# Seven block products for eight in half of a decoder layer's input projection

## The chip, the cores and the metric

The kernel runs on one core of a Trainium2 chip. The metric is the device time of one execution in microseconds (us): before the change the median of three runs is 1809.89 us (1809.57 to 1810.76). The engines are named as the profile names them: PE is TensorE (matmul), PEld its weight loads, DVE is VectorE, ACT is ScalarE, POOL is GpSimd, SP is SyncE, which here only issues DMAs.

## The reference

One layer of a hybrid decoder over 1024 tokens of 2048 channels, in float32. What bears on the change is the first matmul:

```python
def hybrid_layer(x, pre_w, post_w, w_in, ...):
    h = rms_norm(x, pre_w)          # 1024 x 2048
    proj = h @ w_in                 # 2048 x 6016: 47 columns of 128
    za, zb, zc, zd, gate = jnp.split(proj, SPLITS, axis=-1)
    ya = rwkv7_mixer(token_shift(za, mu), ...)   # columns 0 to 12, a scan over the tokens
    yb = swa_sink_attention(zb, sinks)           # 13 to 18
    yc = pool_mixer(zc, pool_w, pool_scale)      # 19 to 22
    yd = spatial_gating(zd, ...)                 # 23 to 30
    y = jnp.concatenate([ya, yb, yc, yd], axis=-1) * jax.nn.silu(gate)   # gate: 31 to 46
    return x + rms_norm(y @ w_out, post_w)
```

RMSNorm divides a token's channels by their root mean square, so its factor (`rstd`) is one number per token, and needs all of the token's channels.

## The kernel before

**Tiling.** The tokens are worked in two halves of 512. The projection makes, for one half, one "column" at a time: 128 output channels x 512 tokens in one PSUM bank, summed over 16 blocks of 128 input channels (`proj`, line 260). Float32 accuracy comes from splitting each operand into a rounded part `hi` and the rest `lo` (`split`, line 161: ScalarE rounds into `wh`, VectorE subtracts into `wl`), and from three matmuls per block (lines 273 to 275: hi x hi, hi x lo, lo x hi), each 128x128 against 128x512. A column so takes 48 matmuls, here called products, and 4 weight splits of 128x512. The split tiles have 3 buffers each, raw weights 3 buffers of 512 KB, and the column's PSUM pool `ps_pj` 2 banks.

**Stages.** `first_half` (line 198) loads and splits the first half of x, and makes columns 12, 0, 4 and 8 at once, while the squares of x are summed for `rstd` (lines 171 to 196). `mixers(0)` (line 876) runs the four mixers of the first half; each mixer is a generator that asks for a column and is stepped once for every column made (the RWKV heads twice). In the first half `rstd` is multiplied in when a column is taken from PSUM (line 889). `out_proj(0)` (line 794) multiplies by `w_out`: 4 x 4 x 16 x 3 = 768 products without other TensorE work, while `second_half` (line 237) scales and splits the second half of x. Then come `mixers(1)` and `out_proj(1)`, and a tail of the last residual rows.

**What sets the order.** A list scheduler places the instructions of each engine when the kernel is built: it takes them as they become ready, by their place in the program, with weight loads and splits ahead (`high_priority`). Each engine then runs its own list strictly in that order. So the RWKV head's work on VectorE (lines 337 to 406, a DMA round trip, the small triangular solve of lines 417 to 421, the chain over 8 chunks of 64 tokens in lines 518 to 545) stands in one list with the weight splits that TensorE's next products wait for.

## Time and profile before

| | us |
|---|---|
| median of 3 runs | 1809.89 |
| the profiled execution's own time | 1808.09 |
| its span, first to last instruction | 1806.3 |
| until the first product | 11.5 |
| from there until the fifth column starts | 52.7 |
| the rest of the first half's projection and mixers | 666.1 |
| output projection, first half | 178.5 |
| projection and mixers, second half | 703.9 |
| output projection, second half | 182.8 |
| tail | 10.8 |

The busy time of an engine is the union of its instructions; an operation that waits in an engine's list is not busy. A matmul's own duration (0.39 us) overlaps with the next one's, so the distance from start to start says what a product costs. PEclk is the clock that TensorE was granted: 1.00 is 2.4 GHz, 0.50 is 1.2 GHz.

### The profile page before, as it was taken

How to read it: one execution, taken by the hardware profiler on the slowest of the kernel's cores; microseconds unless marked ns; L12 is line 12 of the kernel's file. 1: busy time of each engine (PE TensorE's matmuls, PEld its weight loads, DVE VectorE, ACT ScalarE, POOL GpSimd, SP SyncE). 2: the span in 40 equal slices, each digit the busy share in tenths (PEclk: the TensorE clock that was granted, in tenths of full speed). 3: DMA queues.
4: the chain of work that ended last, by engine and by line, in shares of the span. 5: the costliest groups of instructions: out<-in, count | busy, mean ns of one | idle time of the engine just before them, and what ended most of it. 6: DMA issues, size and time to landing. Idle time of an engine off the chain costs nothing.

```text
span 1806.3 us, 26854 instructions
## 1 busy us (share of the span) xinstructions
PE 1754.0 (97%) x10352; PEld 1344.7 (74%) x10352; DVE 988.4 (55%) x2186; ACT 614.9 (34%) x1205; POOL 347.8 (19%) x506
## 2 busy tenths in 40 slices
PE   7999999999999999999999999999999999999997
PEld 5787677767767777788887876677677678778875
DVE  6654677576456644753345457754763564463335
ACT  6333333433333322533233243333333323242230
POOL 4111232022034310110002213311220220100002
PEclk9899999999998999999999999999999999999999
DMA  6242123223323312454343533352232132224445
GB/s 207 91 120 78 59 66 86 70 62 101 105 71 107 114 59 71 145 169 123 123 126 101 174 111 94 103 152 70 73 110 71 59 100 74 71 82 128 140 137 201
DMA packets 58144, 190.00 MB, mean 105 GB/s; under 512 B 8400, under 2 KB 8400, under 8 KB 58016
## 3 DMA queue, kind: packets, MB, share of 16 engines
q1 hardware_dynamic: 44672, 147.34, 26.5%
q0 software_dynamic: 13200, 40.91, 8.0%
q8 instruction: 81, 1.33, 0.3%
q14 instruction: 47, 0.39, 0.1%
q10 hardware_dynamic: 144, 0.03, 0.0%
HBM read 168.86 MB, written 18.87 MB: 104 GB/s over the span
## 4 chain that ended last, share of the span: by engine, by line
PE 83%; DVE 9%; issue 3%; DMA 3%; ACT 1%; POOL 1%; DVEq 0%; SPq 0%; POOLq 0%; ACTq 0%
PE ps_pj L273 18%; PE ps_pj L274 17%; PE ps_pj L275 17%; PE ps_pj L779 3%; PE ps_pj L781 3%; PE ps_pj L780 3%; PE ps_pr L780 3%; PE ps_pr L781 3%; PE ps_pr L779 3%; DVE wl L163 1%; PE ps_pr L401 1%; PE ps_pr L444 1%; DVE ftmp L419 1%; PE ps_y L515 1%; PE ps_ot L653 1%
## 5 line engine op out<-in xcount | busy, mean ns | idle before, releaser
L163 DVE TENSOR_TENSOR wl<-wr,wh 128x512 fp32r<-128x512 f32 x488 | 344.2, 706 | 507.2 <-ACT wh L162 490.6
L273 PE MATMUL ps_pj<-g,wh 128*128 128x512 f32 x1472 | 601.5, 409 | 11.7 <-ACT g L212 11.6
L275 PE MATMUL ps_pj<-g,wl 128*128 128x512 f32 x1472 | 593.6, 403 | 5.7 <-DVE wl L163 5.7
L274 PE MATMUL ps_pj<-g,wh 128*128 128x512 f32 x1472 | 594.0, 404 | 0.0
L162 ACT CAST wh<-wr 128x512 fp32r<-128x512 f32 x488 | 301.6, 620 | 849.7 <-PE ps_pj L274 618.9
L273 PEld LDWEIGHTS ps_pj<-g,wh 128*128 128x128 f32 x1472 | 280.9, 191 | 84.1 <-ACT g L212 11.7
L275 PEld LDWEIGHTS ps_pj<-g,wl 128*128 128x128 f32 x1472 | 280.4, 190 | 74.5 <-DVE wl L163 7.4
L274 PEld LDWEIGHTS ps_pj<-g,wh 128*128 128x128 f32 x1472 | 280.7, 191 | 67.4 <-issue 5.3
L526 POOL TENSOR_SCALAR SD<-g,g 64x64 f32<-64x64 f32 x128 | 63.6, 497 | 502.6 <-DVE g L539 347.5
L779 PE MATMUL ps_pj<-wh,g 128*128 128x512 f32 x224 | 88.5, 395 | 0.5 <-DVE g L889 0.3
L780 PE MATMUL ps_pr<-wl,g 128*128 128x512 f32 x224 | 88.4, 395 | 0.0
L781 PE MATMUL ps_pr<-wh,g 128*128 128x512 f32 x224 | 88.3, 394 | 0.0
L780 PE MATMUL ps_pj<-wl,g 128*128 128x512 f32 x224 | 88.3, 394 | 0.0
L781 PE MATMUL ps_pj<-wh,g 128*128 128x512 f32 x224 | 88.3, 395 | 0.0
L779 PE MATMUL ps_pr<-wh,g 128*128 128x512 f32 x224 | 88.2, 394 | 0.0
L821 POOL DMA_DIRECT2D dram_o<-g x24 | 13.0, 541 | 245.8 <-DVE g L791 242.5
L889 DVE TENSOR_TENSOR g<-ps_pj,g 128x512 f32<-128x512 f32 x45 | 30.9, 687 | 45.6 <-PE ps_pj L275 44.9
L419 DVE TENSOR_TENSOR ftmp<-t,LB 64x1 f32<-64x1 f32 (+14 forms) x120 | 46.1, 384 | 16.8 <-DMA LB<-dl 13.6
L539 DVE SCALAR_TENSOR_TENSOR g<-ps_ch,g,SD 64x64 f32<-64x64 f32 x112 | 31.7, 283 | 34.6 <-PE ps_ch L536 29.9
L779 PEld LDWEIGHTS ps_pj<-wh,g 128*128 128x128 f32 x224 | 42.2, 188 | 11.0 <-DVE g L889 0.7
L779 PEld LDWEIGHTS ps_pr<-wh,g 128*128 128x128 f32 x224 | 42.2, 188 | 10.6 <-DVE g L791 0.8
L781 PEld LDWEIGHTS ps_pj<-wh,g 128*128 128x128 f32 x224 | 42.1, 188 | 9.8
(239 smaller groups left out, 2071.9 us busy)
## 6 DMA issues: line engine op xcount, KB each, us to landing
wr<-in_w_in SPq DMA_DIRECT2D x188, 512.0 KB, 3.8
wr<-in_w_out SPq DMA_DIRECT2D x64, 512.0 KB, 3.6
g<-in_xT POOLq DMA_DIRECT2D x32, 256.0 KB, 6.1
g<-in_x POOLq DMA_DIRECT2D x32, 256.0 KB, 4.6
out_y<-g SPq DMA_DIRECT2D x32, 256.0 KB, 4.0
dram_o<-g POOLq DMA_DIRECT2D x24, 256.0 KB, 3.6
g<-dram_o POOLq DMA_DIRECT2D x24, 256.0 KB, 4.0
g<-in_xT SPq DMA_DIRECT2D x16, 256.0 KB, 5.9
```

Source lines behind the costliest of these rows:

```text
L162: self.nc.scalar.copy(out=hi, in_=raw)
L163: self.nc.vector.tensor_tensor(out=lo, in0=raw, in1=hi.bitcast(F32), op=ALU.subtract)
L273: nc.tensor.matmul(p, hi[:, kk], hh, start=k == 0, stop=False)
L274: nc.tensor.matmul(p, hi[:, kk], hl, start=False, stop=False)
L275: nc.tensor.matmul(p, lo[:, kk], hh, start=False, stop=k == KT - 1)
L419: nc.vector.tensor_tensor(out=tmp[:, 0:i, 0:i], in0=T16[:, 0:i, 0:i].rearrange("p j c -> p c j"), in1=LB[:, 0:i, i].unsqueeze(1).to_broadc ...
L526: nc.gpsimd.tensor_scalar(out=SD[H[h]], in0=SV[h][H[h], c], scalar1=E[H[h], c, C:C + 1], scalar2=None, op0=ALU.mult)
L539: nc.vector.scalar_tensor_tensor(out=SV[h][H[h], c + 1], in0=pt[H[h], 2], scalar=E[H[h], c, C:C + 1], in1=SD[H[h]], op0=ALU.mult, op1=ALU.add)
L779: nc.tensor.matmul(p, yh[:, ms], hi, start=k == 0, stop=False)
L780: nc.tensor.matmul(p, yh[:, ms], lo, start=False, stop=False)
L781: nc.tensor.matmul(p, yl[:, ms], hi, start=False, stop=k == KT - 1)
L889: self.nc.vector.tensor_tensor(out=t, in0=p, in1=self.rstd[0], op=ALU.mult)
```

## The change

The input channels are cut in two halves of eight blocks. For channel blocks 8 to 15 the projection stays as it was, column by column and half by half (24 products a column). For blocks 0 to 7 it is done ahead of all mixers and for both token halves at once, in the scheme of Strassen and Winograd: two columns (m1, m2), two channel quarters and two token halves form a 2 x 2 block product, and seven block products of 12 matmuls stand for eight. The weights' sums and differences (`combine`) are made per pair on VectorE, those of x once (`operands`); 23 pairs and one single column (`solo`, four block products) make the 47 columns. Their results wait in DRAM (`part`), and `column` loads one and adds it as it takes the column's other half from PSUM. Since `rstd` of both token halves is needed for this, x of the second half is loaded at the start as well; meanwhile the other channel half of 12 columns of the first token half is made (`AHEAD`) and also stored to DRAM (`rest`).

```diff
+KH = 4
+SK = 2 * KH
+AHEAD = (12, 0, 4, 8, 1, 5, 9, 2, 6, 10, 3, 7)
+SOLO = 12
...
-        self.gp = pool("gen", 78)
-        self.wrp = pool("wraw", 3)
+        self.gp = pool("gen", 66)
+        self.wrp = pool("wraw", 5)
+        self.wsp = pool("wsum", 4)
+        self.evp = pool("evac", 5)
...
+        self.part = [[self.dpc.tile([P, T], F32, name=f"part{m}_{hf}") for hf in range(NHALF)] for m in range(MT)]
+        self.rest = {m: self.dpc.tile([P, T], F32, name=f"rest{m}") for m in AHEAD}
...
-    def first_half(self):
+    def begin(self):
...
+        for k in range(SK, KT):
+            if k in (SK, SK + 4):
+                self.early[AHEAD[(k - SK) // 4]] = self.w_load(AHEAD[(k - SK) // 4], 1)
             with self.tc.high_priority():
+                xb.append(self.x_load(0, k, nc.sync))
...
+        self.xa = [[], []]
+        with self.tc.high_priority():
+            self.xa[0] = [self.x_load(0, k, nc.sync) for k in range(SK)]
         accs = [self.g(), self.g()]
...
         rstd = self.x_rstd(0, accs)
-        for m, pl in ((12, self.ps_pj), (0, self.ps_pj), (4, self.ps_pr), (8, self.ps_pr)):
-            self.ahead[m] = self.proj(m, pl)
+        held = []
+        def evacuate():
+            m, p = held.pop(0)
+            t = self.tile(self.evp, [P, T], "ev")
+            nc.vector.tensor_tensor(out=t, in0=p, in1=self.rstd[0], op=ALU.mult)
+            nc.gpsimd.dma_start(out=self.rest[m], in_=t)
+        for i, m in enumerate(AHEAD):
+            held.append((m, self.proj(m, (self.ps_pj, self.ps_pr)[i // 2 % 2])))
+            if i == 2:
                 for _ in rstd:
                     pass
+                accs = [self.g(), self.g()]
+                xb = []
+                for k in range(KT):
+                    x = self.x_load(1, (k + SK) % KT, nc.sync)
+                    if k >= KT - SK:
+                        self.xa[1].append(x)
+                    self.x_square(k, x, accs)
+            if i >= 2:
+                evacuate()
+            if i == 5:
+                for _ in self.x_rstd(1, accs):
+                    pass
+                self.operands()
+        while held:
+            evacuate()
+
+    def operands(self):
+        nc = self.nc
+        names = ("b11", "b21", "b22", "t1", "t2", "t3", "t4")
+        self.ops = {n: [] for n in names}
+        for kk in range(KH):
+            b11, b21, b12, b22 = (self.xa[hf][kk + KH * i] for hf in range(2) for i in range(2))
+            for hf, (x, y) in enumerate(((b11, b21), (b12, b22))):
+                for t, k in ((x, kk), (y, kk + KH)):
+                    nc.vector.scalar_tensor_tensor(out=t, in0=t, scalar=self.v["pre_norm_w"][:, k:k + 1],
+                                                   in1=self.rstd[hf], op0=ALU.mult, op1=ALU.mult)
+            t1, t2, t4 = self.g(), self.g(), self.g()
+            nc.vector.tensor_tensor(out=t1, in0=b12, in1=b11, op=ALU.subtract)
+            nc.vector.tensor_tensor(out=t2, in0=b22, in1=t1, op=ALU.subtract)
+            t3 = b12
+            nc.gpsimd.tensor_tensor(out=t3, in0=b22, in1=b12, op=ALU.subtract)
+            nc.gpsimd.tensor_tensor(out=t4, in0=b21, in1=t2, op=ALU.subtract)
+            for n, x in zip(names, (b11, b21, b22, t1, t2, t3, t4)):
+                hi, lo = self.g(dt=F32R), self.g(dt=F32R)
+                self.split(x, hi, lo)
+                self.ops[n].append((hi, lo))
+
+    def strassen(self):
+        nc, tt = self.nc, self.nc.vector.tensor_tensor
+        def combine(op, a, b):
+            with self.tc.high_priority():
+                s = self.tile(self.wsp, [P, T], "ws")
+                tt(out=s, in0=a, in1=b, op=op)
+            return s
+        def product(p, w, name, first):
+            with self.tc.high_priority():
+                hi = self.tile(self.whp, [P, KH, P], "wh", F32R)
+                lo = self.tile(self.wlp, [P, KH, P], "wl", F32R)
+                self.split(w, hi.rearrange("p a b -> p (a b)"), lo.rearrange("p a b -> p (a b)"))
+            for kk, (hh, hl) in enumerate(self.ops[name]):
+                last = kk == KH - 1
+                nc.tensor.matmul(p, hi[:, kk], hh, start=first and kk == 0, stop=False, skip_group_check=True)
+                nc.tensor.matmul(p, hi[:, kk], hl, start=False, stop=False, skip_group_check=True)
+                nc.tensor.matmul(p, lo[:, kk], hh, start=False, stop=last, skip_group_check=True)
+        def evac():
+            return self.tile(self.evp, [P, T], "ev")
+        def copy(p):
+            t = evac()
+            nc.scalar.copy(out=t, in_=p)
+            return t
+        def store(m, hf, t):
+            nc.gpsimd.dma_start(out=self.part[m][hf], in_=t)
+        def add(c, p, m, hf):
+            tt(out=c, in0=p, in1=c, op=ALU.add)
+            store(m, hf, c)
+        def pair(m1, m2):
+            r1, r2 = self.w_load(m1, 0), self.w_load(m2, 0)
+            a11, a12, a21, a22 = r1[:, 0], r1[:, 1], r2[:, 0], r2[:, 1]
+            x, y, z = self.ps(self.ps_pj), self.ps(self.ps_pr), self.ps(self.ps_ot)
+            product(x, a11, "b11", True)
+            c1 = copy(x)
+            product(z, a12, "b21", True)
+            add(c1, z, m1, 0)
+            yield
+            s1 = combine(ALU.add, a21, a22)
+            s2 = combine(ALU.subtract, s1, a11)
+            product(x, s2, "t2", False)
+            c2 = copy(x)
+            product(y, s1, "t1", True)
+            s3 = combine(ALU.subtract, a11, a21)
+            product(x, s3, "t3", False)
+            c3 = copy(x)
+            add(c3, y, m2, 1)
+            yield
+            s4 = combine(ALU.subtract, a12, s2)
+            product(y, s4, "b22", False)
+            add(c2, y, m1, 1)
+            product(x, a22, "t4", False)
+            store(m2, 0, copy(x))
+        def solo(m):
+            r = self.w_load(m, 0)
+            x, z = self.ps(self.ps_pj), self.ps(self.ps_ot)
+            product(x, r[:, 0], "b11", True)
+            c1 = copy(x)
+            product(z, r[:, 1], "b21", True)
+            add(c1, z, m, 0)
+            product(x, r[:, 0], "t1", False)
+            product(x, r[:, 1], "b22", False)
+            store(m, 1, copy(x))
+        solo(SOLO)
+        ms = [m for m in range(MT) if m != SOLO]
+        before = None
+        for i in range(0, len(ms), 2):
+            now = pair(ms[i], ms[i + 1])
+            next(now)
+            if before is not None:
+                for _ in before:
+                    pass
+            next(now)
+            before = now
+        for _ in before:
+            pass
...
-    def second_half(self):
+    def half_input(self, hf):
...
-        for k in range(KT + 2):
-            if k < KT:
-                xs.append(self.x_load(1, k))
+        h, xs, n = [], [], KT - SK
+        for i in range(n + 2):
+            if i < n:
+                xs.append(self.x_load(hf, SK + i))
...
     def proj(self, m, pl=None):
...
-        for half in range(2):
-            raw = self.ahead.pop((m, half), None) or self.w_load(m, half)
-            for q in range(2):
...
+        raw = self.early.pop(m, None) or self.w_load(m, 1)
+        for q in range(2):
...
+    def column(self, hf, m):
+        with self.tc.high_priority():
+            part = self.tile(self.evp, [P, T], "ev")
+            self.nc.sync.dma_start(out=part, in_=self.part[m][hf])
+        t = self.g()
+        if hf == 0 and m in self.rest:
+            self.nc.sync.dma_start(out=t, in_=self.rest[m])
+            self.nc.gpsimd.tensor_tensor(out=t, in0=t, in1=part, op=ALU.add)
+        else:
+            self.nc.vector.tensor_tensor(out=t, in0=self.proj(m), in1=part, op=ALU.add)
+        return t
...
             def proj(r):
-                p = self.ahead.pop(r.want, None) or self.proj(r.want)
-                if hf == 0:
-                    t = self.g()
-                    self.nc.vector.tensor_tensor(out=t, in0=p, in1=self.rstd[0], op=ALU.mult)
-                    p = t
-                r.want = r.gen.send(p)
+                r.want = r.gen.send(self.column(hf, r.want))
...
     def run(self):
-        self.first_half()
+        self.begin()
...
-        self.mixers(0, self.x_stats(1), 30)
-        ssq = self.out_proj(0, self.second_half())
+        self.strassen()
+        for _ in self.half_input(0):
+            pass
+        self.mixers(0, iter(()), 30)
+        ssq = self.out_proj(0, self.half_input(1))
         self.mixers(1, self.finish(0, ssq), 4)
         self.out_proj(1)
```

`x_load` loses its rule on queues (x of both halves now goes over SP at the start, over POOL in `half_input`), the 32 loads of x for the second half become 16 at the start and 8 later (8 more for the first half), and in the tail a few tiles move from the pool `gen` to the new pools `evac` and `wsum`.

**Where instructions move.** In the changed program the lines have other numbers: L409 to L411 are the products of `proj`, L302 to L304 those of `product`, L175 is the VectorE half of `split` (L163 before), L200 and L206 are the small matmuls of `x_rstd` (lines 188 and 194 before), L424 is the addition in `column`.

TensorE before, at the end of the fourth column, which was made ahead (`ps_pr_518`), and at the start of the fifth:

```order
L273 MATMUL ps_pr_518<-g_225,wh_571 128x512
L274 MATMUL ps_pr_518<-g_226,wh_571 128x512
L275 MATMUL ps_pr_518<-g_225,wl_572 128x512
L273 MATMUL ps_pr_518<-g_229,wh_571 128x512
L274 MATMUL ps_pr_518<-g_230,wh_571 128x512
L275 MATMUL ps_pr_518<-g_229,wl_572 128x512
L330 MATMUL ps_pr_634<-g_607,g_605 128x512
L273 MATMUL ps_pj_687<-g_169,wh_690 128x512
L274 MATMUL ps_pj_687<-g_170,wh_690 128x512
L275 MATMUL ps_pj_687<-g_169,wl_691 128x512
L273 MATMUL ps_pj_687<-g_173,wh_690 128x512
```

TensorE now, at the end of the twelfth column made ahead (`ps_pr_1073`) and at the start of the block products, where `ps_pj_1129` and `ps_ot_1130` are the first two sums of `solo`, `ps_ot_691` the sums of the squares of the second token half and `ps_ot_720` its `rstd`:

```order
L200 MATMUL ps_ot_691<-ones,g_496 128x1
L200 MATMUL ps_ot_691<-ones,g_497 128x1
L409 MATMUL ps_pr_1073<-g_293,wh_1092 128x512
L410 MATMUL ps_pr_1073<-g_294,wh_1092 128x512
L411 MATMUL ps_pr_1073<-g_293,wl_1093 128x512
L206 MATMUL ps_ot_720<-shapes,ny_718 128x128 x4
L302 MATMUL ps_pj_1129<-g_738,wh_1131 128x512
L302 MATMUL ps_ot_1130<-g_742,wh_1149 128x512
L303 MATMUL ps_pj_1129<-g_739,wh_1131 128x512
L304 MATMUL ps_pj_1129<-g_738,wl_1132 128x512
L303 MATMUL ps_ot_1130<-g_743,wh_1149 128x512
```

Before, products follow products. Now the `rstd` of the second token half is finished right behind the last column made ahead, and the next products read x as scaled with it (`g_738`, `g_742`). On VectorE these stand in between, from the first scaling by that `rstd` on, 39 operations up to the `lo` part of the last block of those two products (`g_860`); the last of them, and the next two:

```order
L175 TENSOR_TENSOR g_829<-g_809,g_828 128x512
L175 TENSOR_TENSOR g_833<-g_810,g_832 128x512
L175 TENSOR_TENSOR g_837<-g_544,g_836 128x512
L175 TENSOR_TENSOR g_841<-g_811,g_840 128x512
L275 TENSOR_TENSOR g_848<-g_549,g_303 128x512
L276 TENSOR_TENSOR g_849<-g_569,g_848 128x512
L175 TENSOR_TENSOR g_856<-g_303,g_855 128x512
L175 TENSOR_TENSOR g_860<-g_311,g_859 128x512
L175 TENSOR_TENSOR g_864<-g_569,g_863 128x512
L175 TENSOR_TENSOR g_868<-g_848,g_867 128x512
```

The list so makes all operands of a block of channels before it goes to the next one (all seven splits, L175, of blocks `g_816` to `g_841`, then the sums and splits of the fourth), and the weight split (`wl`) comes behind.

VectorE in `mixers(0)` before, at a place where an RWKV head's chunk products are prepared (L367, L368, L374) and attention scores are scaled (L612, L617):

```order
L163 TENSOR_TENSOR wl_2181<-wr_2178,wh_2180 128x512
L368 TENSOR_TENSOR g_1942<-g_1935,g_1925 64x4x64
L374 SCALAR_TENSOR_TENSOR g_1947<-g_1523,drv,g_1920 64x4x64
L374 SCALAR_TENSOR_TENSOR g_1948<-g_1523,drv,g_1920 64x4x64
L374 SCALAR_TENSOR_TENSOR g_1949<-g_1523,drv,g_1920 64x4x64
L374 SCALAR_TENSOR_TENSOR g_1950<-g_1523,drv,g_1920 64x4x64
L163 TENSOR_TENSOR wl_2197<-wr_2178,wh_2196 128x512
L612 SCALAR_TENSOR_TENSOR g_1965<-shapes,ps_ot_1959 128x256 x2
L612 SCALAR_TENSOR_TENSOR g_1968<-shapes,ps_ot_1960 128x256 x2
L617 TENSOR_REDUCE mx_1971<-g_1965 128x2
L163 TENSOR_TENSOR wl_2215<-wr_2212,wh_2214 128x512
L617 TENSOR_REDUCE mx_1971<-g_1968 128x2
L889 TENSOR_TENSOR g_2060<-ps_pj_1991,g_516 128x512
```

VectorE now at the same place (L517 and L523 are the old L368 and L374, L761 and L766 the old L612 and L617):

```order
L517 TENSOR_TENSOR g_5459<-g_5452,g_5442 64x4x64
L523 SCALAR_TENSOR_TENSOR g_5464<-g_5238,drv,g_5437 64x4x64
L523 SCALAR_TENSOR_TENSOR g_5465<-g_5238,drv,g_5437 64x4x64
L523 SCALAR_TENSOR_TENSOR g_5466<-g_5238,drv,g_5437 64x4x64
L523 SCALAR_TENSOR_TENSOR g_5467<-g_5238,drv,g_5437 64x4x64
L761 SCALAR_TENSOR_TENSOR g_5482<-shapes,ps_ot_5476 128x256 x2
L761 SCALAR_TENSOR_TENSOR g_5485<-shapes,ps_ot_5477 128x256 x2
L766 TENSOR_REDUCE mx_5488<-g_5482 128x2
L766 TENSOR_REDUCE mx_5488<-g_5485 128x2
L424 TENSOR_TENSOR g_5510<-ps_pj_5511,ev_5508 128x512
```

Before, a weight split (`wl`) stood between every few of these operations. Now none stands among them: the last one is 33 rows ahead of this piece (with the small chain operations between), the next one 15 rows behind it, and 56 rows of VectorE's list stand between the two.

## Rows read from the trace of the kernel before

**Rows 1.** The page: busy time, granted clock in 40 slices, the chain that ended last.

```profile
PE 1754.0 (97%) x10352; PEld 1344.7 (74%) x10352; DVE 988.4 (55%) x2186; ACT 614.9 (34%) x1205; POOL 347.8 (19%) x506
...
PEclk9899999999998999999999999999999999999999
...
PE 83%; DVE 9%; issue 3%; DMA 3%; ACT 1%; POOL 1%; DVEq 0%; SPq 0%; POOLq 0%; ACTq 0%
```

**Rows 2.** Windows by stage: length, busy (instructions) of each engine, clock, DMA.

```profile
core 0: us, PE busy (x) PEld busy (x) DVE busy (x) ACT busy (x) POOL busy (x), PEclk, DMA share, GB/s
0.00:11.50 11.50, 0.00 (x0) 0.00 (x0) 3.13 (x14) 3.85 (x7) 4.68 (x14) 1.00 0.85 260
11.50:64.20 52.70, 51.90 (x218) 40.25 (x218) 38.57 (x62) 30.68 (x53) 17.03 (x17) 1.00 0.52 173
64.20:730.30 666.10, 650.20 (x4195) 489.53 (x4195) 394.16 (x916) 228.16 (x454) 152.29 (x206) 0.97 0.28 82
730.30:908.80 178.50, 178.23 (x770) 144.18 (x769) 83.74 (x129) 64.83 (x122) 16.64 (x32) 1.00 0.45 141
908.80:1612.70 703.90, 693.31 (x4406) 527.27 (x4405) 387.44 (x908) 232.52 (x465) 138.39 (x204) 0.98 0.33 98
1612.70:1795.50 182.80, 180.10 (x770) 143.45 (x768) 75.94 (x145) 54.19 (x105) 18.74 (x35) 1.00 0.47 146
1795.50:1806.30 10.80, 0.29 (x2) 0.00 (x0) 5.39 (x18) 0.69 (x2) 0.00 (x0) 0.67 0.55 210
```

**Rows 3.** Groups by line: name, shapes, count, busy us, mean ns, idle before.

```profile
L273 PE MATMUL ps_pj<-g,wh 128*128 128x512 f32 x1472 | 601.5, 409 | 11.7 <-ACT g L212 11.6 <-ACT wh L162 0.2
...
L163 DVE TENSOR_TENSOR wl<-wr,wh 128x512 fp32r<-128x512 f32 x488 | 344.2, 706 | 507.2 <-ACT wh L162 490.6 <-PE ps_pj L275 10.9 <-PE ps_ot L755 2.1
L162 ACT CAST wh<-wr 128x512 fp32r<-128x512 f32 x488 | 301.6, 620 | 849.7 <-PE ps_pj L274 618.9 <-PE ps_pr L781 182.7 <-issue 21.1
...
L889 DVE TENSOR_TENSOR g<-ps_pj,g 128x512 f32<-128x512 f32 x45 | 30.9, 687 | 45.6 <-PE ps_pj L275 44.9 <-ACT g L196 0.7
```

**Rows 4.** Groups by line: splitting and scaling x, DMA issue, evacuation on ScalarE.

```profile
L163 DVE TENSOR_TENSOR g<-g,g 128x512 fp32r<-128x512 f32 x48 | 32.4, 715 | 4.0 <-ACT g L162 3.8
...
L821 POOL DMA_DIRECT2D dram_o<-g x24 | 13.0, 541 | 245.8 <-DVE g L791 242.5 <-issue 2.1 <-DVE nv L147 0.7
...
L245 DVE SCALAR_TENSOR_TENSOR g<-g,sv,g 128x512 f32<-128x512 f32 x16 | 11.8, 746 | 2.4 <-DMA g<-in_xT 2.4
...
L790 ACT ACTIVATE g<-ps_pj 128x512 f32<-128x512 f32 x18 | 10.8, 598 | 36.1 <-PE ps_pj L781 35.6
```

**Rows 5.** Line 180 on both its engines: ns min/median/max, first and last start.

```profile
L180 POOL TENSOR_TENSOR g<-g,g x22: 1259/1300/1818, 26.9 to 624.4; 128x512 f32<-128x512 f32 x22
...
L180 DVE TENSOR_TENSOR g<-g,g x7: 685/1593/1820, 28.7 to 41.0; 128x512 f32<-128x512 f32 x7
```

**Rows 6.** Groups by line: an RWKV head's preparation on VectorE.

```profile
L368 DVE TENSOR_TENSOR g<-g,g 64x256 f32<-64x256 f32 x32 | 21.2, 663 | 0.0
...
L374 DVE SCALAR_TENSOR_TENSOR g<-g,drv,g 64x256 f32<-64x256 f32 x32 | 15.0, 506 | 0.3
```

**Rows 7.** Window of one column whose VectorE sum is the larger, columns as in Rows 2.

```profile
250.60:265.40 14.80, 14.80 (x90) 11.27 (x90) 11.95 (x38) 3.00 (x6) 5.55 (x7) 1.00 0.26 59
```

**Rows 8.** Windows before and in two stretches of lower clock, columns as in Rows 2.

```profile
536.30:543.10 6.80, 5.08 (x64) 4.08 (x62) 6.71 (x11) 1.87 (x3) 4.61 (x6) 1.00 0.13 35
543.10:556.80 13.70, 13.70 (x62) 9.59 (x63) 7.02 (x18) 4.72 (x8) 9.13 (x10) 0.50 0.32 99
1198.50:1205.30 6.80, 6.80 (x115) 5.12 (x113) 3.95 (x9) 1.49 (x3) 0.00 (x0) 1.00 0.26 80
1205.30:1208.70 3.40, 3.40 (x14) 2.68 (x11) 3.10 (x8) 0.00 (x0) 0.00 (x0) 0.51 0.00 0
```

**Rows 9.** Timeline of TensorE: start us, length us, line, at 1.2 GHz.

```profile
13.37 0.63 PE L273 MATMUL ps_pj<-g,wh 128*128 128x512 f32 x1
13.80 0.63 PE L274 MATMUL ps_pj<-g,wh 128*128 128x512 f32 x1
```

69 lines of the change are left out of this document (27 added, 42 removed).

## The prediction

> **What bounds the kernel now.** I read the page first: TensorE is busy 97% of the span, and the chain that ended last runs 83% on TensorE [rows 1]. Then the windows by stage: TensorE is busy 178.2 of 178.5 us in an output projection, 650.2 of 666.1 and 693.3 of 703.9 us in the two mixer stages, while VectorE is busy 394.2 and 387.4 us there, little over half [rows 2]. So products set the time, and a product's price comes from the stage that has nothing else: 178.5 us / 768 = 0.232 us. Of the rest of TensorE's busy time, 2064 products of the first mixer stage (43 columns of 48) at 0.232 are 478.8 us, which leaves 171.4; in the second, 2256 are 523.4 and leave 169.9. These some 170 us a stage are the mixers' own small matmuls and the time lost at the lower clock.
>
> **What is removed.** Before: 2 x 47 x 48 = 4512 products (line 273, a third of them, has 1472 in `ps_pj` [rows 3], and 32 for two columns in `ps_pr`). After: 12 columns ahead x 24 = 288, `solo` 4 x 12 = 48, pairs 23 x 7 x 12 = 1932, the other channel half 35 x 24 = 840 and 47 x 24 = 1128; together 4236. 276 fewer x 0.232 = 64.0 us, if TensorE stays the bound everywhere. Weight splits go from 376 to 24 + 165 + 164 = 353. The question is where this saving is lost: half the products leave the mixer stages, and with them the cover under which VectorE does the mixers' work.
>
> **Stage by stage, against the span of 1806.3.**
>
> Start, 11.5 us: the same loads end it. Kept.
>
> Columns made ahead: 288 x 0.232 = 66.8. Before, the first 192 (44.5) took 52.7 us, 8.2 more, for loads and the low clock at the start [rows 2]; VectorE has the additions of squares and 12 evacuations here, for which I add 3: 78 us (72 to 88).
>
> Operands of x: the `rstd` of the second half stands behind the twelfth column in TensorE's order, and 39 VectorE operations lie between it and the last product of the first two sums: 8 scalings x 0.746, 23 splits x 0.715 [rows 4], 8 subtractions x 0.706 (the nearest row is the split, also two float32 inputs from SBUF [rows 3]) = 6.0 + 16.4 + 5.6 = 28.0 us. TensorE has 24 products in it, 5.6 us: it stands idle for 22.4. The 8 GpSimd subtractions beside them cost more: in line 180, VectorE's additions took 685 ns at best and 1593 at the median, while GpSimd did the same operation [rows 5]; 8 x 0.9 = 7.3 us if all collide, nothing if none; I take 2.6, so 25 us (15 to 32). The Trainium skill (SBUF — State Buffer, "Who interferes with whom") says that a VectorE operation with two SBUF inputs and a GpSimd one that reads SBUF exclude each other for a whole instruction; the rows of line 180 agree, and by the rule alone this term would be 30.
>
> Block products: 1980 x 0.232 = 459.4 us. A pair takes TensorE 84 x 0.232 = 19.5 us. Beside it VectorE has 7 splits, 4 sums (priced as splits) and 3 additions: 11 x 0.706 + 3 x 0.687 = 9.8; ScalarE 7 x 0.620 + 4 x 0.598 = 6.7; GpSimd four DMA issues, 2.2 us [rows 3, 4]. DMA moves 2 x 512 + 4 x 256 KB per pair, 108 GB/s, against 260 in the first window [rows 2]. Every split stands two products of 12 ahead in its list. So TensorE is the bound; bounds 455 to 480.
>
> First mixer stage: TensorE 840 x 0.232 = 194.9 + 171.4 = 366.3 us. VectorE: 394.2, less 172 splits x 0.706 (121.4) and 46 evacuations x 0.687 (31.6), is 241; plus 70 splits (49.4), 35 additions of `column` (24.0) and 8 scalings and splits of x (11.7) is 326. On the whole TensorE has still a little more. But the two are not spread alike. I laid the durations of before along the changed order, from each column's first product to the next one's: VectorE's sum is over TensorE's in 14 of 34 columns, by 35 us together; the same count for before gives 6 us, and a stage time within 3%. The second piece of VectorE's order shows why: no split among the head's preparation (lines 367, 368, 374 at 0.684 to 0.506 us [rows 6]). In the mixer stages before, VectorE's longest stretch without a weight split is 9.2 us by these durations; now this stage has five over 10 (27.7, 23.2, 19.4, 15.4, 12.8), 98.5 us, in which TensorE has 37 us of small matmuls and, with three split buffers, 3 x 12 products or 8.4 us of work each time: 98.5 - 37 - 42 = 20 us idle at least. I take 32 (20 to 35), as these stretches follow each other closely and leave the buffers empty. Idle of before without that share: 15.9 - 6.4 = 9.5. Together 408 us.
>
> Output projections: 178.5 and 182.8, unchanged; the first has 8 scalings of x fewer, which TensorE hid.
>
> Second mixer stage: TensorE 1128 x 0.232 = 261.7 + 169.9 = 431.6. VectorE 387.4 - 133.6 + 94 x 0.706 + 47 x 0.687 = 352. The column count gives 26 us of excess, but only one stretch over 10 us without a split (13.2), which the buffers and its own small matmuls can cover: 0 to 26, I take 20. Idle 10.6 - 2.0 = 8.6. Together 460.
>
> Tail 10.8 (-1 to +3 for the smaller pool). The loads and stores of `part` and `rest` are hidden: 56 MB over the run beside 25 MB fewer weights.
>
> Sum: 11.5 + 78 + 25 + 459.4 + 408 + 178.5 + 460 + 182.8 + 10.8 = 1814.0 us of span. The profiled execution took 1808.09, 1.8 over its span, and the median of the runs lies 1.8 over that: 1818 us, 0.4% over 1809.89. So of the 64 us nothing is left: 25 go to the operands, 44 to VectorE's excess (32 + 20, less the 8 of before), 3 to the start.
>
> **Rivals.**
>
> The saving shows (not slower). If the scheduler's list runs in fact with the buffers full before each stretch, the first stage loses only the 20 us and the second none, and the operand gap is 13 because TensorE reaches it late: 1818 - 12 - 20 - 12 = 1774. For it: in a column of before whose VectorE sum is 17.4 us for TensorE's 14.3, TensorE was busy throughout and the column took 14.8 [rows 7]; a single excess is hidden. Against it: it is now up to 10 us in a column, and columns with an excess follow each other. It decides as soon as the stages and the gap together come out 12 us under the forecast.
>
> The clock. TensorE fell to 1.2 GHz for 13.7 us after 6.8 us with 64 matmuls, most of them small, busy 5.1 us; and also after 6.8 us in which it was busy throughout with 115, nearly all small [rows 8]. At that level products start 0.43 us apart [rows 9]. Before, the two stages had a mean clock of 0.97 and 0.98 [rows 2]. Products now are 840 in 408 us for 2064 in 666, so such stretches come more often: if another fifth of the 1968 products runs there, 394 x 0.20 = 79 us, a third of it under VectorE's excess: 1818 + 53 = 1871. The Trainium skill (TensorE: Matmul & The Clock Gate, "What's actually happening") puts the low clock down to idleness of TensorE; the second window fell without any, so here idle is not the only cause, and by the page alone this rival would be smaller.
>
> Block products not TensorE-bound. If one split of each pair comes 1 us late, through an evacuation that stands ahead of it on VectorE, 23 us: 1841. The lists speak against it.
>
> **How the numbers follow.** Forecast 0.40 (1800 to 1836), of which 0.08 is faster by over 0.2%, 0.10 within it, 0.22 slower; 0.2%, some 3.6 us, is about what a measurement of this kernel can tell from no change. The saving shows 0.33, all faster (1755 to 1800). The clock 0.20, slower (1845 to 1900). Late splits 0.07, slower. That is faster 0.41, same 0.10, slower 0.49. Leaving a tenth on either side, the range is 1760 to 1880.
>
> **What would show it.** In the changed kernel's profile: 0.23 us from product to product through the block products, 19.5 us a pair with TensorE at 99% and VectorE near half; a hole of some 25 us in TensorE before them, its releaser VectorE's split in `operands`; in the first mixer stage (about 408 us) TensorE busy near 90% and VectorE over 75%, TensorE's waits ended by the `wl` split and by the addition in `column`; the second at about 460 us. It is wrong if the pairs take over 20.5 us, if the mean clock of a mixer stage is under 0.93, or if the stages come out at their TensorE sums of 366 and 432.

## The result, and the profile after

The change makes the kernel slower: 1977.88 us median (1973.6 to 1982.8) against 1809.73 for the kernel before, ratio 1.0931, 95% interval [1.0904, 1.0958]. That is 160 us over the forecast and outside its range. The page of the changed kernel (span 1977.0 us), in the lines that answer to [rows 1]:

```profile
PE 1778.8 (90%) x10084; PEld 1356.4 (69%) x10084; DVE 1141.4 (58%) x2423; ACT 662.6 (34%) x1296; POOL 415.4 (21%) x608
...
PEclk9959999999997888978899999997989978999999
...
PE 74%; DVE 11%; issue 6%; DMA 4%; POOL 3%; ACT 2%; SPq 0%; POOLq 0%; DVEq 0%; ACTq 0%
```

TensorE has 268 instructions fewer and is busy longer (1778.8 us for 1754.0), and its clock, which was under 0.9 in two of the 40 slices before, is so in twelve. The windows of the changed kernel by stage (columns as in [rows 2]) are: columns made ahead, block products, first mixer stage, second mixer stage:

```profile
10.50:114.10 103.60, 86.44 (x337) 68.41 (x337) 58.86 (x96) 38.22 (x67) 26.40 (x26) 0.86 0.52 175
114.10:605.10 491.00, 469.95 (x1983) 375.26 (x1984) 259.12 (x382) 166.85 (x293) 74.93 (x118) 0.96 0.32 107
605.10:1088.20 483.10, 401.57 (x2955) 288.35 (x2953) 311.41 (x800) 158.79 (x340) 136.92 (x187) 0.85 0.29 84
1268.80:1784.10 515.30, 460.09 (x3276) 333.03 (x3274) 350.68 (x859) 177.34 (x368) 138.27 (x203) 0.92 0.36 110
```

| stage | forecast us | measured us | difference |
|---|---|---|---|
| start | 11.5 | 10.5 | -1 |
| columns ahead, operands, block products | 78 + 25 + 459.4 | 103.6 + 491.0 | +32 |
| first mixer stage | 408 | 483.1 | +75 |
| second mixer stage | 460 | 515.3 | +55 |
| output projections and tail | 372.1 | 373.5 | +1 |

So 130 of the 163 us are in the two mixer stages. TensorE's busy time there is 401.6 + 460.1 = 861.7 us where its sums were 366.3 + 431.6 = 797.9: 64 us more for the same instructions (35 in the first stage, 28 in the second). Its idle time (length less busy) is 81.5 + 55.2 = 136.7 us where 70 were allowed: 67 us more. The mean clocks of 0.85 and 0.92 mean that 30% and 16% of the two stages ran at 1.2 GHz, some 227 us, where [rows 2] give 6% and 4%, some 68.

What TensorE waits for in the first mixer stage (changed kernel; us in total, times, longest):

```profile
PE ps_pr L533 <- ACT g L500: 15.5, 1, 15.5
PE ps_pr L550 <- DVE g L523: 14.5, 4, 4.7
PE ps_pr L714 <- POOL g L707: 10.3, 4, 4.8
PE ps_ch L685 <- DVE g L682: 6.2, 5, 1.9
PE ps_pr L593 <- POOL g L582: 6.0, 1, 6.0
PE ps_pj L409 <- DVE g L424: 5.8, 4, 3.1
```

All but the last are small matmuls of the RWKV heads (banks `ps_pr`, `ps_ch`). In neither mixer stage does a product wait for a weight split; what products wait for most is the addition in `column` that frees their bank (L424: 5.8 us here, 8.7 in the second stage). Each wait of the heads goes back to a chain, that is, to operations that follow from one another over several engines: ScalarE's square in a head's preparation, VectorE's L523, GpSimd's normalisation. In the kernel before, the first of a block's three products waited 11.7 us in the whole run, 11.6 of it for the splits of x at the start [rows 3].

### The profile page after: what moved, and what is told of

Its sections match the earlier page's. It is cut to its first block, busy times and chain, and to the rows that moved or that the text cites. A ratio compares the mean times of both kernels' runs of the same rounds, so it can differ in the third digit from the quotient of the medians.

```text
span 1977.0 us, 27197 instructions
## 1 busy us (share of the span) xinstructions
PE 1778.8 (90%) x10084; PEld 1356.4 (69%) x10084; DVE 1141.4 (58%) x2423; ACT 662.6 (34%) x1296; POOL 415.4 (21%) x608
## 4 chain that ended last, share of the span: by engine, by line
PE 74%; DVE 11%; issue 6%; DMA 4%; POOL 3%; ACT 2%; SPq 0%; POOLq 0%; DVEq 0%; ACTq 0%
PE ps_pj L409 7%; PE ps_pj L410 7%; PE ps_pj L411 6%; PE ps_pj L304 4%; PE ps_pj L302 4%; PE ps_pj L303 4%; PE ps_pj L928 3%; PE ps_pj L929 3%; PE ps_pj L930 3%; PE ps_pr L928 3%; PE ps_pr L930 3%; PE ps_pr L929 3%; PE ps_pr L302 2%; PE ps_pr L304 2%; PE ps_pr L303 2%
## 5 line engine op out<-in xcount | busy, mean ns | idle before, releaser
L175 DVE TENSOR_TENSOR wl<-wr,wh 128x512 fp32r<-128x512 f32 x373 | 268.7, 721 | 369.9 <-ACT wh L174 358.0
L174 ACT CAST wh<-wr 128x512 fp32r<-128x512 f32 x373 | 231.1, 620 | 646.0 <-PE ps_pj L410 279.3
L409 PE MATMUL ps_pj<-g,wh 128*128 128x512 f32 x704 | 304.7, 433 | 35.5 <-DVE g L424 14.4
L410 PE MATMUL ps_pj<-g,wh 128*128 128x512 f32 x704 | 300.4, 427 | 0.6 <-DVE g L225 0.6
L411 PE MATMUL ps_pj<-g,wl 128*128 128x512 f32 x704 | 295.6, 420 | 0.0
L409 PEld LDWEIGHTS ps_pj<-g,wh 128*128 128x128 f32 x704 | 140.7, 200 | 76.3 <-issue 16.4
L303 PE MATMUL ps_pj<-g,wh 128*128 128x512 f32 x380 | 152.0, 400 | 19.4 <-DVE g L175 19.4
L410 PEld LDWEIGHTS ps_pj<-g,wh 128*128 128x128 f32 x704 | 140.3, 199 | 33.7 <-DVE g L225 2.2
L411 PEld LDWEIGHTS ps_pj<-g,wl 128*128 128x128 f32 x704 | 139.9, 199 | 34.1 <-issue 4.6
L302 PE MATMUL ps_pj<-g,wh 128*128 128x512 f32 x380 | 151.7, 399 | 1.5 <-ACT g L174 1.2
L304 PE MATMUL ps_pj<-g,wl 128*128 128x512 f32 x380 | 151.8, 400 | 0.3 <-DVE wl L175 0.3
L315 POOL DMA_DIRECT2D part<-ev x94 | 50.8, 541 | 397.7 <-DVE ev L318 337.3
L174 ACT CAST wh<-ws 128x512 fp32r<-128x512 f32 x92 | 57.2, 622 | 176.6 <-PE ps_pj L303 96.2
L175 DVE TENSOR_TENSOR wl<-ws,wh 128x512 fp32r<-128x512 f32 x92 | 63.2, 687 | 73.0 <-ACT wh L174 73.0
L303 PEld LDWEIGHTS ps_pj<-g,wh 128*128 128x128 f32 x380 | 72.1, 190 | 39.2 <-DVE g L175 22.0
```

What stands on the lines that cost most here:

```text
L174: self.nc.scalar.copy(out=hi, in_=raw)
L175: self.nc.vector.tensor_tensor(out=lo, in0=raw, in1=hi.bitcast(F32), op=ALU.subtract)
L302: nc.tensor.matmul(p, hi[:, kk], hh, start=first and kk == 0, stop=False, skip_group_check=True)
L303: nc.tensor.matmul(p, hi[:, kk], hl, start=False, stop=False, skip_group_check=True)
L304: nc.tensor.matmul(p, lo[:, kk], hh, start=False, stop=last, skip_group_check=True)
L409: nc.tensor.matmul(p, hi[:, kk], hh, start=k == 0, stop=False)
```

## The experiments

**The scheme in its own stage.** Seven block products were turned back into eight:

```diff
+        def column(m):
...
+            for q, names in enumerate((("b11", "b12"), ("b21", "b22"))):
...
+                for p, n in zip((x, y), names):
...
-            now = pair(ms[i], ms[i + 1])
...
+            column(m)
```

> Only the block stage is changed: every column's channel blocks 0 to 7 are made for both token halves by ordinary products, eight block products where the changed kernel has seven; the sums of weights and of x fall away. 2256 products there for 1980: 276 x 0.232 = 64.0 us more TensorE work. Theory A (the saving is real in its own stage and the loss is elsewhere, in mixers that have lost half their products): the stage takes 491 + 64, less some 10 for a shorter list of operands, and the rest stays as it is: about 2032 us (2020 to 2045). Theory B (the seven products bring their own cost, by the additions of weights or the waiting banks): the stage grows by less than 30 and the time is under 2005.

Measured: 2009.9 us (1.1127 [1.111, 1.1144]), between the two theories: 5 us over Theory B's bound and 10 under Theory A's. The time grows by 32 us and the block stage by 38, more than B's 30 and less than A's 54. TensorE's own work decides for A's reading of the products, not for its number. The block stage of this run:

```profile
109.20:638.50 529.30, 527.53 (x2257) 424.77 (x2258) 89.40 (x133) 120.51 (x210) 56.41 (x104) 1.00 0.29 99
```

TensorE's busy time is 527.5 us for 470.0: the scheme saves 57.6 us of TensorE work, nearly the 64.0 priced (against the run e13 below, whose block stage runs at full clock as this one does, it is 62.9). It then loses 19 of them to idle time (1.8 us here, 21.0 there) among its first products. The mixer stages stay at 480 and 519 us. The saving is real; the loss is elsewhere.

**How many products stand beside the mixers.** Three runs change nothing but that number, in both mixer stages. The new lines below are those of e2 (36 a column), e11 (48) and e9 (6), in this order; the flags that start and end a sum go with them:

```diff
-            for kk in range(4):
+            for kk in list(range(4)) * (2 if q == 0 and pl is None else 1):
...
+            for kk in list(range(4)) * (2 if pl is None else 1):
...
+            for kk in range(4 if pl is not None else 1):
```

> The changed kernel, with the first 12 products of every column in both mixer stages issued twice (the second pass starts the sum anew, so the first one is work for nothing): 35 x 12 + 47 x 12 = 984 products, 228 us of TensorE work at 0.232, with no further split, load or wait. Theory A (TensorE's idle time and lower clock in the mixers are missing cover: any product in that place fills them): the stages go to their TensorE sums, 366 + 97 and 432 + 131, plus the idle of the kernel before, some 475 and 575 for 483 and 516 now: about 2029 us (2010 to 2060), granted clock of both stages at 0.95 or more. Theory C (the time is lost at waits that stand at fixed places in the list whatever is around them): the 228 us come on top, 2150 to 2206.

> The changed kernel with all 24 products of every column in the mixers issued twice (48 as before the change; the second quarter is so counted twice in the sums): no other work. TensorE's sums are 561 and 693 us. Theory A: the stages come to these sums plus the 17 and 11 us idle of the kernel before: 578 and 704, 2260 us in all (2245 to 2280), granted clock 0.97 or more. Theory F (the additions and loads of `part` delay TensorE whatever stands beside them): each stage stays 40 us or more above its sum, over 2300 us.

> The changed kernel with only 3 of the 12 products behind each weight split in the two mixer stages (6 a column instead of 24; these columns are incomplete sums); weight loads, splits and additions stay. TensorE's own sums there are 220 and 235 us, VectorE's amounts 311 and 351. Theory A (chains: operations that follow from one another, longer than any one engine's amount): the stages stop well above VectorE's amounts, at 420 to 470 us each, 1840 to 1930 us in all. Theory V (VectorE's amount is what is left): the stages come within 20 us of VectorE's busy time, some 330 and 370: about 1680 us.

Measured: 2066.82 us, 2257.67 us and 2008.09 us. The windows of the two mixer stages, e9 (6 products a column):

```profile
602.00:1110.50 508.50, 324.61 (x2326) 219.29 (x2324) 312.62 (x800) 157.30 (x339) 137.15 (x188) 0.59 0.27 79
1290.80:1810.30 519.50, 343.25 (x2431) 232.38 (x2429) 350.01 (x860) 175.47 (x368) 139.15 (x203) 0.64 0.37 109
```

e2 (36):

```profile
601.40:1107.50 506.10, 472.32 (x3375) 344.74 (x3373) 315.95 (x799) 158.41 (x339) 137.97 (x187) 0.95 0.28 80
1286.20:1872.40 586.20, 566.81 (x3840) 422.50 (x3840) 348.58 (x859) 178.26 (x367) 135.21 (x203) 0.97 0.32 97
```

and e11 (48):

```profile
600.00:1176.90 576.90, 558.12 (x3794) 413.73 (x3794) 317.05 (x802) 160.53 (x341) 139.96 (x191) 0.99 0.23 70
1355.50:2061.80 706.30, 693.28 (x4405) 525.05 (x4405) 353.75 (x862) 180.76 (x371) 137.33 (x204) 0.98 0.27 81
```

| products a column | TensorE's sums us | stages us | over the sums us | clock |
|---|---|---|---|---|
| 6 | 220 and 235 | 508.5 and 519.5 | 288 and 284 | 0.59, 0.64 |
| 24 (the change) | 366 and 432 | 483.1 and 515.3 | 117 and 84 | 0.85, 0.92 |
| 36 | 464 and 562 | 506.1 and 586.2 | 42 and 24 | 0.95, 0.97 |
| 48 | 561 and 693 | 576.9 and 706.3 | 16 and 13 | 0.99, 0.98 |

The sums are worked out as in the forecast (0.232 us a product, plus 171.4 and 169.9). VectorE does the same work in all four: 311 to 317 and 349 to 354 us. Read from below, the stages have a floor near 480 and 515 us, a length that fewer products do not take them under. With 630 and 846 products fewer than in the changed kernel, e9 takes 25 and 4 us more; its clock of 0.59 and 0.64, TensorE mostly at 1.2 GHz, is the likely reason, though no run shows that by itself. Read from above, the time follows TensorE's sum only while that lies well over the floor. At 48 products the changed kernel's mixers are within 3 us of the 16 and 11 us that the kernel before lost, so its loads and additions of `part` cost next to nothing as long as the products are there. That is Theory A, and e11 came out as it says (2257.67 for 2245 to 2280); e2 fell 7 us outside its range (2066.8 for 2010 to 2060), and e9 came above what either theory gave.

**The same without the change.** The kernel before, with half of its products, weight loads and weight splits left out of the mixers:

```diff
-        for half in range(2):
+        for half in range(0 if pl else 1, 2):
...
-                    nc.tensor.matmul(p, hi[:, kk], hh, start=k == 0, stop=False)
+                    nc.tensor.matmul(p, hi[:, kk], hh, start=k == (0 if pl else 8), stop=False)
```

> The kernel before, with the products and splits of channel blocks 0 to 7 left out of every column from the fifth on (24 products a column in the mixers; the columns are incomplete sums): no block products, no sums, no loads of `part`, no second addition, the old start. TensorE's sums are 411 us (first mixer stage, 43 columns) and 432. Theory A (the loss comes from half the products being gone, whatever became of them): the stages lose about what they lose in the changed kernel (117 and 84 us): 528 and 515, 1480 us in all (1440 to 1500). Theory F (it comes from what the change added: additions, loads and columns without products): 425 and 445, about 1310 us.

Measured: 1426.73 us. The two mixer stages:

```profile
63.60:554.50 490.90, 438.16 (x3162) 317.07 (x3162) 338.63 (x829) 173.47 (x367) 147.98 (x204) 0.91 0.22 66
735.20:1230.60 495.40, 453.89 (x3278) 331.49 (x3276) 322.12 (x814) 173.18 (x369) 137.49 (x203) 0.92 0.30 90
```

80 and 64 us over the sums of 411 and 432, where the changed kernel has 117 and 84, and the kernel before 16 and 11. So 144 of 201 us, some seven tenths, come without anything that the change adds; counted from the 27 us of before, 117 of 174. The time lies 13 us under Theory A's range. The other 57 us no run takes apart: the first stage has 1032 products here for 840 there, and the change adds VectorE's additions and columns that come from DRAM.

**VectorE's share.** Without VectorE's half of the weight split in the mixers, at 24 and at 6 products a column:

```diff
-                self.split(raw[:, q], hi.rearrange("p a b -> p (a b)"), lo.rearrange("p a b -> p (a b)"))
+                if pl is not None or self.lok is None:
...
+                else:
+                    lo = self.lok
+                    nc.scalar.copy(out=hi.rearrange("p a b -> p (a b)"), in_=raw[:, q])
```

> The changed kernel without the VectorE half of the weight split in the two mixer stages: the rounded rest of the first weight tile is kept and used for all columns, so these stages compute something else. VectorE loses 163 subtractions of 0.72 us, 117 us in two stages that have 311 and 351; TensorE's work is the same. Theory V (as forecast: TensorE waits because VectorE has more work than TensorE in many stretches): the excess goes, the mixers come near 420 and 460, 1890 to 1930 us. Theory A2 (TensorE waits for the length of the mixers' own chains, operation after operation over VectorE, GpSimd, ScalarE and DMA, and not for the amount of VectorE's work): under 25 us are gained, 1953 to 1978.

> The changed kernel with 6 products a column in the mixers, as in the run e9, and without VectorE's half of the weight splits there, as in e3 (both leave out part of the computation). VectorE's amounts fall from 313 and 350 us to some 268 and 290. Theory V (the floor of 508 and 519 us is VectorE's amount plus its fixed waits): the stages fall by as much, to 465 and 458: about 1905 us. Theory K (the floor is the heads' chain, on a TensorE that runs at 1.2 GHz for most of the stage): they fall by less than 20 us each, 1968 us or more.

Measured: e3 1930.23 us (1.0705 [1.0653, 1.0758]), at the edge of Theory V's range, 41 us under the changed kernel by the two ratios; e14 1930.86 us, between the two theories. e3's mixer stages:

```profile
601.80:1064.80 463.00, 395.18 (x2954) 284.76 (x2953) 267.70 (x732) 157.79 (x340) 134.34 (x187) 0.87 0.29 87
1245.80:1732.40 486.60, 449.69 (x3277) 327.85 (x3275) 289.94 (x768) 176.03 (x368) 133.33 (x203) 0.93 0.38 116
```

and e14's:

```profile
602.20:1072.20 470.00, 308.09 (x2324) 213.72 (x2323) 265.24 (x731) 156.12 (x339) 134.98 (x187) 0.63 0.28 84
1252.60:1735.60 483.00, 337.42 (x2430) 227.33 (x2429) 289.51 (x767) 174.53 (x369) 136.32 (x203) 0.66 0.38 117
```

In e3 VectorE has 44 and 61 us less, and the stages are 20 and 29 us shorter: not quite half of each microsecond, and far from the 420 and 460 us that Theory V gave them. At the floor (e14 against e9) 47 and 61 us less give 38 and 36. So VectorE's amount bears on the floor, but 162 and 146 us of TensorE's idle time are left there with VectorE busy only 56% and 60%. That the rest is waiting from one operation of a chain to the next fits TensorE's waits above; no run shows it by itself. The two runs also differ by 1476 products, 342 us at 0.232, and end within 1 us of each other: without these splits, 18 products a column more are free.

**The operands of x.** e4 makes the two that need only the first token half (b11, b21) early; e13 also goes operand by operand in place of block by block:

```diff
+                self.operands_first()
...
-            for n, x in zip(names, (b11, b21, b22, t1, t2, t3, t4)):
...
+            self.operand("t1", t1[kk])
+        for kk in range(KH):
+            self.operand("b22", self.scaled(1, kk + KH))
+        for kk in range(KH):
...
+            self.operand("t2", t2[kk])
...
```

The first line is in both runs, the others are e13's.

> The changed kernel with x's operands in two steps: the two that need only the first token half (b11, b21) are scaled and split as soon as that half's factor is there, during the columns made ahead; 8 scalings and 8 splits less stand between the second factor and the block products. Theory G (the gap of 19.4 us ahead of the block products, and the lower clock in and after it, come from the 39 VectorE operations in a row): the first block products start at once, the gap falls under 6 us, and 25 to 35 us are gained: about 1948 us. Theory H (what the operations lose there they take from the columns made ahead, where VectorE has the squares, or the gap comes back at the third product, which needs t1): under 12 us, 1966 to 1978.

> The changed kernel with x's operands made one after another over all four channel blocks (b11 and b21 after the first factor; then t1, b22, t2, t3, t4, in the order in which TensorE asks for them), where the changed kernel makes all seven operands of a channel block before the next. Theory G2 (the earlier try kept its gap since t1 of the last block stood behind five other operands): TensorE's idle time in the block stage falls from 21 to under 8 us, and the lower clock ahead of it and in it from 68 to under 40 us: 1945 to 1960 us. Theory H2 (VectorE needs its 26 us for these operands in any order, and TensorE uses them up at once): 1964 us or more.

In the changed kernel the gap is one row of TensorE's waits:

```profile
PE ps_pj L303 <- DVE g L175: 19.4, 4, 5.7
```

e4 took 1968.95 us (1.0899 [1.0883, 1.0915]), as Theory H said. The gap came back at `t1`, which the third product of `solo` needs, and with it 18.9 us idle in the block stage:

```profile
PE ps_pj L315 <- DVE g L175: 7.8, 3, 2.6
PE ps_pj L314 <- ACT g L174: 7.5, 3, 3.7
```

e13 took 1958.22 us (1.0851 [1.0814, 1.0888]), as Theory G2 said, 20 us under the changed kernel by the medians, 14 by the ratios. Its columns ahead and block stage:

```profile
10.40:107.30 96.90, 79.78 (x329) 63.39 (x330) 57.99 (x93) 40.51 (x72) 25.22 (x24) 0.89 0.52 182
107.30:581.20 473.90, 464.67 (x1992) 372.73 (x1991) 255.88 (x385) 163.50 (x288) 74.54 (x120) 1.00 0.33 112
```

The block stage is 17 us shorter than in the changed kernel, at a clock of 1.00. It was the order in which operands were made, not their amount.

**Holes that move.** Four runs leave all amounts as they are and try to rearrange the first mixer stage:

```diff
+            with self.tc.high_priority():
+                self.nc.sync.dma_start(out=t, in_=self.rest[m])
...
+            part = self.g() if late else self.tile(self.evp, [P, T], "ev")
...
+AHEAD = tuple(range(31, 43))
...
+PERIOD = 9
...
+                for _ in range(2 - tick % 2):
```

These are, in this order, e5 (the load of `rest` moved up), e12 (own buffers for `part`), e6 (other columns made ahead) and e7 (the heads spread out).

> The changed kernel with the load of `rest` (the other half of a column made ahead) put at the same priority as that of `part`, so that SyncE's queue holds the two side by side. Before this edit a `part` load of a later column, which waits for a buffer that an earlier column's addition must free, stands ahead of the `rest` load that this addition waits for: in the first mixer stage three columns of the first RWKV head follow each other at 4.7 us, and TensorE stands 15.5 us (its longest wait) for what comes of them. Theory S (SyncE's order makes that wait): it falls under 8 us, the stage gains 7 to 15 us: about 1967 us. Theory N (the head's preparation on VectorE and ScalarE is as long anyway, or the loads take it): under 4 us, 1974 to 1980.

> The changed kernel with `part` of the twelve columns made ahead loaded into tiles of the pool gen, so that in SyncE's queue the loads of `part` and `rest` of the first head's columns stand side by side and none waits for the addition of the column ahead of it. Theory S (the 4.7 us from column to column, and with them TensorE's wait of 15.5 us, come from the queue's order): that wait falls to 8 us or less, 6 to 15 us are gained: 1963 to 1972 us. Theory N (other chains are as long there): within 4 us of 1978.

> The changed kernel with other columns made ahead: twelve gate columns (31 to 42) in place of the RWKV heads' twelve. The same number of products in every stage; in the first mixer stage the heads' columns now come with their 24 products, and the gates' without. Theory A (what counts is how much product work lies beside the heads' chains): the stage's idle time falls from 81 to some 55 us and its lower clock with it, 25 to 40 us are gained: about 1945 us. Theory A0 (the chains run through the whole stage, and the cover that the heads get at the front is missing behind): within 10 us of 1978, the holes only move.

> The changed kernel with the RWKV heads stepped three times per two columns (2 and 1 by turns, in place of 2 per column), and started every 9 columns in place of 10: a column now has half the products, so two steps of a head follow each other in half the time; this spreads a head over some 19 columns instead of 14. Amounts of work are unchanged on every engine. Theory L (TensorE waits since the head's operations, which follow from one another over four engines and DMA, are asked for too soon): idle time in the stages falls from 81 and 55 us to 50 and 30, with it the lower clock, 50 to 80 us are gained: 1900 to 1930 us. Theory V (VectorE's amount is the limit): VectorE does the same, under 20 us: 1958 or more. If the heads end after the last column, the stage's end loses its products, and the time rises over 1978.

Measured: 1976.41, 1976.16, 1987.84 and 1990.5 us (ratios 1.0944 [1.0901, 1.0987], 1.0957 [1.0919, 1.0994], 1.1006 [1.0971, 1.1042], 1.1013 [1.0965, 1.1061]). None gains, and e6 and e7 are some 0.7% slower than the changed kernel. That is against Theory A of e6 and Theory L of e7; A0 holds at the edge of its 10 us. In e7 the stage ends 8 us behind its last product, as in the changed kernel, so the late end that was named there is not its loss. e5 left SyncE's order as it was and so tests nothing. e12 did change it. GpSimd's additions of `part` and `rest` in the changed kernel, with the idle time ahead of each in brackets:

```profile
617.50 1.27 POOL L422 TENSOR_TENSOR g<-g,ev 128x512 f32<-128x512 f32 x1 [6.36 <-DMA g<-rest]
622.28 1.26 POOL L422 TENSOR_TENSOR g<-g,ev 128x512 f32<-128x512 f32 x1 [3.50 <-DMA g<-rest]
626.89 1.26 POOL L422 TENSOR_TENSOR g<-g,ev 128x512 f32<-128x512 f32 x1 [3.35 <-DMA g<-rest]
```

follow each other at 4.7 us, each behind a load that SyncE issued only when the one before had freed a buffer. In e12 these additions are no longer 4.7 us apart, and the wait of 15.5 us fell to 7.6, as Theory S said; but the time is Theory N's, and another wait grew from 14.5 to 20.9:

```profile
PE ps_pr L551 <- DVE g L524: 20.9, 4, 5.8
...
PE ps_pr L534 <- ACT g L501: 7.6, 1, 7.6
```

In e6 the longest wait is another one, for L582's product on GpSimd:

```profile
PE ps_pr L593 <- POOL g L582: 22.0, 2, 21.7
```

In e7 one of 15.9 us stays, and one of 15.7 us, for L707's product, joins it:

```profile
PE ps_pr L714 <- POOL g L707: 27.6, 3, 15.7
PE ps_pr L533 <- ACT g L500: 15.9, 1, 15.9
```

The stage stays between 481 and 500 us in all four (483.1 in the changed kernel): a hole that was closed opened elsewhere.

**Half the size.** Channel blocks 0 to 3 in place of 0 to 7, 36 products a column in the mixers (e8); then with e13's order and e12's buffers (e15):

```diff
-KH = 4
+KH = 2
-AHEAD = (12, 0, 4, 8, 1, 5, 9, 2, 6, 10, 3, 7)
+AHEAD = (12, 0, 4, 8, 1, 5, 9, 2)
...
```

> The change at half its size: only channel blocks 0 to 3 (a quarter of the channels) go through seven block products, of 6 matmuls each; columns in the mixers keep 36 of 48 products, 8 columns are made ahead instead of 12. Products: ahead 8 x 36 = 288, blocks 990, mixers 39 x 36 = 1404 and 47 x 36 = 1692, in all 138 fewer than before the change (32 us). Theory A (cover): with 36 products a column the stages lose what they lost in the run with doubled first products, 42 and 23 us over their TensorE sums of 497 and 562: 11 + 115 + 230 + 539 + 181 + 585 + 182 + 11 = 1854 us (1830 to 1875). Theory F (the loss comes with the restructuring as such: the additions of `part`, the loads, the columns without products): the stages lose as much as in the changed kernel, 117 and 84 us: about 1990 us.

> The change at half its size (run e8: 1860 us), with operands made one after another as in e13 and own buffers for the loads of `part` as in e12. By the gaps of e8 (idle 10 us in the block stage, 27 us of lower clock there and ahead of it, a wait of 9 us for the first head): 12 to 30 us less, 1830 to 1848 us. Below 1810, the kernel before, only if the mixer stages gain 30 us besides, for which no run speaks.

Measured: 1859.68 us (1.0294 [1.0255, 1.0332]) for e8, 6 us over Theory A's 1854 and in its range, and 1836.77 us (1.0168 [1.0134, 1.0203]) for e15, in its range too. The mixer stages of e15:

```profile
342.40:866.80 524.40, 503.66 (x3519) 367.30 (x3518) 339.20 (x839) 184.47 (x381) 126.73 (x180) 0.96 0.31 96
1045.90:1644.20 598.30, 572.06 (x3841) 423.75 (x3840) 382.95 (x907) 206.67 (x416) 137.95 (x203) 0.96 0.38 116
```

27 and 36 us over the sums of 497 and 562, together 63 where the kernel before has 27: these 36 us alone are more than the 32 that this size saves. It is the best form of the change found, and 1.7% slower than the kernel before.

## Why the prediction was wrong

**Right: the price of the scheme.** A pair was put at 19.5 us; in the trace pairs follow each other at 19.47 us. Without the gap (e13) the block stage has 464.7 us busy for the 459.4 forecast. The output projections and the tail came out within 2.1 us each.

**Right in place, short in size: the operands.** The gap was seen (25 us forecast, 21.0 us idle in the block stage, ended by VectorE's split). What was missed is its neighbour. The columns ahead took 103.6 us for 78: 17.2 idle, most of it at the sums of squares and the factors (L200, L206), and a clock of 0.86; the block stage began at the lower clock as well (0.96 over the stage). e13 takes 24 us from the two stages together. For the start of the kernel before, the forecast took a low clock from [rows 2], which gives 1.00 there; what speaks for it is the 0.43 us from product to product in [rows 9].

**Wrong: the two mixer stages.** The step that failed laid VectorE's and TensorE's durations of each column side by side, took the larger, and added the idle time of before (408 and 460 us). What it read from VectorE's list was there: five stretches of over 10 us without a weight split (windows of the changed kernel, columns as in [rows 2]):

```profile
844.90:879.00 34.10, 26.43 (x181) 20.26 (x182) 26.77 (x66) 10.20 (x25) 12.30 (x17) 0.60 0.10 30
719.90:751.10 31.20, 23.64 (x159) 17.36 (x157) 23.05 (x61) 9.85 (x26) 14.09 (x20) 0.62 0.10 31
620.90:651.20 30.30, 12.53 (x79) 10.29 (x80) 17.43 (x41) 6.95 (x11) 9.45 (x11) 0.57 0.19 57
963.50:984.90 21.40, 16.69 (x98) 12.29 (x99) 14.56 (x36) 2.56 (x6) 7.17 (x10) 0.68 0.11 32
768.40:780.50 12.10, 8.57 (x53) 6.22 (x54) 11.30 (x44) 3.34 (x12) 5.92 (x7) 0.72 0.08 24
```

VectorE is busy 93 us in them (98.5 forecast), and TensorE stands idle 41 (32 taken). But the other 40 us of idle time in this stage, and all but 6 of the 55 in the second, lie outside such stretches, where 9.5 and 8.6 us were allowed; and TensorE's busy time is 35 and 28 us over its sums, which the forecast took over at the clock of before. Its sum has no term for a stage's own length. With 6 products a column it would have forecast VectorE's amounts, 313 and 350 us, and the runs show 508.5 and 519.5. The idle time of before (16 and 11 us) was no constant to be carried over: it was what 48 products a column left uncovered. The excess of VectorE that the forecast did price is part of it, as e3 shows, but TensorE stood mostly at small matmuls behind chains. Of the two causes forecast for its waits, the `wl` split ended none and the addition in `column` 5.8 and 8.7 us. TensorE was busy 83% of the first stage and VectorE 64%, where near 90% and over 75% were to show the forecast right.

**The clock was a rival and came on top.** The rival's 53 us (1871) are near the 64 us that TensorE's same instructions took longer. It was put beside the forecast as another case, though its cause, too few products, is the forecast's own. By the forecast's own sign (a mixer stage under 0.93) it is refuted at 0.85 and 0.92. The clock ahead of and in two of these stretches (changed kernel, columns as in [rows 8]):

```profile
613.20:620.00 6.80, 3.88 (x15) 2.05 (x14) 1.92 (x6) 2.17 (x4) 1.27 (x1) 1.00 0.71 230
620.00:647.30 27.30, 8.63 (x58) 7.21 (x59) 16.46 (x37) 5.70 (x10) 8.11 (x9) 0.50 0.18 57
801.00:807.80 6.80, 6.80 (x117) 4.73 (x116) 5.01 (x13) 2.19 (x6) 0.00 (x0) 0.99 0.39 116
807.80:811.20 3.40, 3.40 (x39) 2.34 (x38) 2.40 (x7) 0.62 (x1) 0.00 (x0) 0.52 0.02 5
```

The first low stretch begins 1.5 us into the wait of 15.5 us (618.5 to 634.0), and TensorE is busy 8.6 us of its 27.3. In the second the clock fell, as in the second pair of [rows 8], while TensorE was busy throughout, with matmuls nearly all of them small. The Trainium skill (TensorE: Matmul & The Clock Gate, "What's actually happening") has the throttled clock as the default that activity releases. The 27.3 us agree; the second stretch has no idle time ahead of it by this profile, and there the trace does not bear the page out.

**What stays open.** How the floor divides between VectorE's amount, the chains' waits and the lower clock: e14 puts some 37 us a stage on VectorE's splits, and no run held the clock up without adding products.

## What to carry to other kernels

Work that is taken from the bound engine is worth its price only in a stage that has nothing else to wait for; in a stage that it shares with chains, it is also the cover of those chains, and the stage has a floor that a profile of the covered kernel does not show. Before such a change, run the kernel with that work thinned out or doubled in place: time against amount shows where the line bends, here where TensorE's sums reach the floor, at some 32 to 38 products a column. When moving waits around changes their names and hardly their sum, as in the four runs here, what is missing is cover; order paid only in the block stage (e13), where one gap stood by itself.
